# Later stores, later gate evictions and other queue places in the attention stage of a gated encoder block

## The chip, the cores and the metric

The kernel runs on one core of a Trainium2 chip. The metric is the device time of one execution in microseconds (us). The engines that matter are TensorE (PE: matmuls and transposes), its weight load (PEld), VectorE (DVE), ScalarE (ACT), GpSimd (POOL) and SyncE (SP, which only issues DMAs). Each works through its own instructions in the order in which they were written; an instruction waits on semaphores of other engines and of DMAs. DMAs are issued by SP and by ACT.

## The reference

One layer of an encoder block over 1024 positions of width 1024, in float32:

```
h = rmsnorm(x, g_mix) * (1 + scale1) + shift1          # shift, scale, gate from silu(c) @ w_ada + b_ada
proj = h @ w_in                                        # q, k, v of branches A and B, gates gA, gB
oa = mixture_of_dilations(qa, ka, va, rel_bias)        # A: 8 heads, three dilated windows each
ob = neighbourhood_attention_2d(qb, kb, vb, na_rpb)    # B: 8 heads, 8 x 16 window on a 16 x 64 grid
merged = sigmoid(ga) * (oa @ w_branch_dil) + sigmoid(gb) * (ob @ w_branch_na)
x = x + gate1 * (merged @ w_out)
h2 = rmsnorm(x, g_ffn) * (1 + scale2) + shift2
u = depthwise_conv(h2 @ w_up);  x = x + gate2 * ((gelu(u_gate) * u_val) @ w_down)
return rmsnorm(x, g_final)

# mixture_of_dilations: for each window, softmax attention with a bias, and its log-denominator;
w = softmax(stack(lses));  out = einsum(w, stack(outs))   # the windows' outputs are weighed and added
```

## The kernel before

Every float32 product is made of three matmuls on high and low parts, so an operand is split by a copy on ACT (the high part) and a subtraction on DVE or POOL (the low part). The changed part is the attention stage. It is written as 102 slots, a table from slot number and phase to jobs. In each slot the kernel first runs `settle` (ACT and DVE work that follows the previous slot's transposes and scores), then the phases "first" (loads and POOL work), "O" (probabilities times values), "T" (transposes of the probabilities), "S" (scores) and "last". PE, ACT, DVE, SP and POOL all take the order in which this is written.

Between the phases, `fill(n)` puts in n steps of the gate projection: three matmuls of 128x512 (L84 to L86) for one of 8 blocks of the contraction. Eight steps make a 128x512 tile `pj` in one of two PSUM banks; there are 32 such tiles, 256 steps. Twenty-one steps are left after the last slot; among them the next stage's operands are prepared (`o_split`, `first_split`): this is the seam. A tile's bank is free when ACT has copied it to `gs` (L1309); ACT then issues the store (L1310).

ACT and DVE work that needs no exact place stands in a list, `aside`. `catch_up` takes from it after each step, and `ensure(mark)` empties it up to a mark.

Branch A runs in slots 0 to 63 (`DilHead`, 8 slots a head, `DilPair` for two heads). Scores get a bias tile that POOL first adds `lnm` to (L853, L990). When a pair is done, its softmax statistics are turned, stored and read back in another layout (L1121 to L1129), factors are computed on DVE, stored (L1150, L1155), read back spread over positions (`fb`, L1162), the sums `u` are multiplied by them (`weigh`, L1167) and added (`merge`, L1176), and the result `oa` is stored (L1177). This runs beside later heads, for the last pair beside branch B.

Branch B (`NaHead`, 4 slots a head from slot 64) loads q and k (L401), values (L773) and a bias for each of three column blocks (L1218, `na_bias`). DVE adds it to the scores (L1240), ACT takes the exponential (L1242), DVE and POOL normalise halves (L1247, L1250), PE transposes (L1259) and multiplies (L1272), ACT and DVE add halves to `u` (L1281, L1285), and after two heads SP stores `ob` (L1287).

Each DMA is given one of eight semaphores in turn, in the program's order over both issuing engines, so an issue also waits for the DMA eight places before it.

Of the kernel before, what the change touches and what calls it, by code (L numbers as in the profile page):

```python
# [29 lines left out]
def hybrid_encoder(tc, xT, c, w_ada, small, w_in, p1_bias, p23_bias, na_bias, ln2_mult, ident, w_br, w_out,  # L30
# [61 lines left out]
    ps_g = tc.alloc_tile_pool(name="psg", bufs=2, space=PSUM)  # L92
    qkpool = tc.alloc_tile_pool(name="qk", bufs=4)

# [859 lines left out]
    slots = collections.defaultdict(lambda: {"first": [], "O": [], "T": [], "late O": [], "S": [], "last": [], "W": []})  # L954

    def at(slot, phase, job, *args):
        slots[slot][phase].append((job, args))

    class DilHead:
# [133 lines left out]
    class DilPair:  # L1093
        def __init__(self, pr):
            self.pr, s0 = pr, 16 * pr
            at(s0, "first", self.begin) if pr else self.begin()
            for i in range(2):
                DilHead(self, pr, i, s0 + 8 * i, lambda: self.u, lambda: self.st)
            at(s0 + 17, "T", self.turn)
            at(s0 + 20, "first", self.spread)  # L1100
            at(s0 + 22, "last", self.factors)
            at(s0 + 23, "last", self.shares)
            for z in range(2):
                at(s0 + 25 + z, "first", self.load, 1, z)
            for n, g, z in ((28, 1, 0), (29, 1, 1), (31, 0, 0), (32, 0, 1)):
                at(s0 + n, "last", self.weigh, g, z)
            at(s0 + 33, "first", self.merge)

# [31 lines left out]
        def shares(self):  # L1140
# [5 lines left out]
            for g in range(2):  # L1146
                dve.tensor_tensor(fa[:, g], fa[:, g], fl, OP.mult)
            to = f_scr[self.pr]
            for i in range(2):
# [14 lines left out]
        def weigh(self, g, z):  # L1164
            ensure(self.done)
            dst = self.u[g][:, 512 * z:512 * z + 512]
            dve.tensor_tensor(dst, dst, self.fb.pop((g, z)), OP.mult)  # L1167
            if g:
                self.load(0, z)

        def merge(self):
            u = self.u
            for z in range(2):
                dst = u[1].rearrange("p (r b j) -> p b r j", r=4, b=8)[:, 4 * z:4 * z + 4]
                src = u[0][:, 512 * z:512 * z + 512].rearrange("p (b r j) -> p b r j", b=4, r=4)
                pool.tensor_tensor(dst, dst, src, OP.add)  # L1176
            sp.dma_start(o_scr[0][self.pr], u[1])  # L1177

    na_col = [0, 576, 576, 1344]

    class NaHead:
        def __init__(self, head, s0):
# [7 lines left out]
            for n, cb in enumerate((0, 3, 1, 2)):  # L1190
                at(s0 + n - 1, "first", self.bias, cb)
                at(s0 + n, "S", self.scores, cb)
# [69 lines left out]
        def out(self, pair):  # L1262
# [20 lines left out]
            def two():  # L1283
                for dst, pv in parts:
                    dve.tensor_tensor(dst, pv[0:64], dst, OP.add)  # L1285
                if self.i and pair == (1, 2):
                    sp.dma_start(o_scr[1][self.head // 2], oT)  # L1287
            o_marks.append(aside(800, one, two))

    def fill_steps():  # L1290
        w, raw = first_w, {1: ahead.pop(25)}
        w_mark = 0
        marks = [0, 0]
        for n in range(16):
# [6 lines left out]
            for hf in range(2):  # L1301
                ensure(marks[-2])
                p = ps_g.tile([128, 512], FT, name="pj")
                for k in range(KT):
                    product(p, w, lambda k: h[hf, k], ks=[k])
                    if k == KT - 1:
                        def out(p=p, n=n, hf=hf):
                            g = gspool.tile([128, 512], FT, name="gs")
                            act.activation(g, p, AF.Copy)  # L1309
                            act.dma_start(g_scr[n][:, halves[hf]], g)  # L1310
                        aside(600, out)
                        marks.append(count[0])
                    yield
# [24 lines left out]
    att_sp.enter_context(tc.manual_schedule(engines={sp.engine}))  # L1338
    fill(5)
    for s in range(102):  # L1340
        n = 2 + (s % 4 == 3) if s < 64 else 2 + s % 2 if s < 96 else 1
        settle()
# [5 lines left out]
        run(slots[s]["last"])  # L1348
        fill(n - (n > 1))
    ensure(count[0])  # L1350
    sm_pool.release()
# [724 lines left out]
```

## Time and profile before

| | us |
|---|---|
| median of 3 runs (lowest to highest) | 1515.66 (1515.45 to 1517.59) |
| the profiled execution, its own time | 1514.76 |
| its span, first to last instruction | 1513.0 |
| PE busy | 1456.3 (96%) |
| DVE, ACT, POOL busy | 965.3, 792.8, 841.3 |
| mean granted clock of PE | 0.987 |
| attention stage, about | 277 to 677 |

How to read it: times are us from the span's start. In a table of windows each engine's busy time in a stretch stands with its count of instructions; the granted clock is PE's, and the DMA share is the packets' time over 16 DMA engines. In a list of waits a row names who waited, for whom, the total, how often, and the longest. In a timeline the brackets give the idle time of the engine just before an instruction and what ended it.

### The profile page before, as it was taken

What the parts mean: (1) busy time and instruction counts of PE and PEld (TensorE: products, weight loads), DVE (VectorE), ACT (ScalarE), POOL (GpSimd) and SP (SyncE); (2) the same over time, 40 slices, a digit from 0 to 9 for tenths busy, and PEclk for the clock granted to TensorE, in tenths of its full rate; (3) what the DMA queues carried; (4) which work ended last, traced back from release to release, by engine and by line L of the source; (5) the groups of instructions that cost most, each with busy time, mean ns of one, the idle gap of its engine ahead of it and who ended that gap; (6) DMA issues with size and microseconds to landing.
All of it is one profiled execution on the core that took longest, in us unless ns stands there. A gap on an engine that the chain in (4) does not pass through costs nothing.

```text
span 1513.0 us, 21241 instructions
## 1 busy us (share of the span) xinstructions
PE 1456.3 (96%) x7308; PEld 1230.2 (81%) x7308; DVE 965.3 (64%) x1809; ACT 792.8 (52%) x1479; POOL 841.3 (56%) x690
## 2 busy tenths in 40 slices
PE   9999999899999789999999999999999999999998
PEld 8877888788888678878888878888888888877888
DVE  7696543256655566656634898666666667787865
ACT  6635543377776456654335455444444447574542
POOL 4165675343342345522258858766666676988712
PEclk9999999999999889999999999999999999999999
DMA  9595355855687979558734412222222234532213
GB/s 369 200 349 200 108 188 204 213 144 148 150 220 210 232 189 265 167 192 274 248 134 153 140 55 98 84 84 85 84 84 84 84 127 142 202 124 80 101 48 112
DMA packets 130515, 241.13 MB, mean 159 GB/s; under 512 B 47812, under 2 KB 60740, under 8 KB 130372
## 3 DMA queue, kind: packets, MB, share of 16 engines
q1 hardware_dynamic: 117144, 211.65, 45.3%
q10 hardware_dynamic: 13264, 28.12, 5.0%
q8 instruction: 58, 0.95, 0.3%
q14 instruction: 49, 0.40, 0.1%
HBM read 185.60 MB, written 59.90 MB: 162 GB/s over the span
## 4 chain that ended last, share of the span: by engine, by line
PE 46%; DVE 3%; DMA 2%; POOL 2%; ACT 1%; issue 1%; SPq 0%; DVEq 0%; POOLq 0%; ACTq 0%
PE pj L495 10%; PE pj L496 10%; PE pj L497 10%; PE pj L86 5%; PE pj L84 5%; PE pj L85 5%; DMA wraw<-w_down 1%; DVE big L460 1%; POOL wsl L61 0%; DVE big L1705 0%; DMA oraw<-ob 0%; ACT wsh L57 0%; DVE op L1606 0%; POOL big L441 0%; ACT whi L57 0%
## 5 line engine op out<-in xcount | busy, mean ns | idle before, releaser
L61 POOL TENSOR_TENSOR wlo<-wraw,whi 128x512 fp32r<-128x512 f32 (+1 forms) x90 | 114.6, 1294 | 133.9 <-ACT whi L57 132.1
L495 PE MATMUL pj<-op,wsh 128*128 128x512 f32 x408 | 158.7, 390 | 2.8 <-ACT wsh L57 2.8
L496 PE MATMUL pj<-op,wsh 128*128 128x512 f32 x408 | 158.7, 389 | 0.5 <-DVE op L1495 0.5
L497 PE MATMUL pj<-op,wsl 128*128 128x512 f32 x408 | 157.4, 389 | 0.0
L61 POOL TENSOR_TENSOR wsl<-big,wsh 128x512 fp32r<-128x512 f32 (+1 forms) x86 | 111.7, 1320 | 44.4 <-ACT wsh L57 39.3
L84 PE MATMUL pj<-h,whi 128*128 128x512 f32 x272 | 118.7, 436 | 2.5 <-ACT gs L1309 2.5
L85 PE MATMUL pj<-h,whi 128*128 128x512 f32 x272 | 109.5, 403 | 0.0
L86 PE MATMUL pj<-h,wlo 128*128 128x512 f32 x272 | 109.4, 402 | 0.0
L1705 DVE SCALAR_TENSOR_TENSOR big<-pj,sm,big 128x512 f32<-128x512 f32 (+2 forms) x183 | 94.9, 563 | 16.5 <-ACT big L1699 15.6
L889 DVE TENSOR_TENSOR tl<-T,th 128x512 fp32r<-128x512 f32 (+3 forms) x120 | 76.3, 650 | 36.5 <-ACT th L885 36.2
L495 PEld LDWEIGHTS pj<-op,wsh 128*128 128x128 f32 x408 | 76.7, 188 | 19.6 <-ACT wsh L57 3.6
L495 PE MATMUL pj<-op,whi 128*128 128x512 f32 x232 | 90.6, 390 | 0.0
L496 PEld LDWEIGHTS pj<-op,wsh 128*128 128x128 f32 x408 | 76.7, 188 | 16.8 <-DVE op L1495 0.9
L497 PE MATMUL pj<-op,wlo 128*128 128x512 f32 x232 | 90.3, 389 | 0.0
L496 PE MATMUL pj<-op,whi 128*128 128x512 f32 x232 | 90.3, 389 | 0.0
L497 PEld LDWEIGHTS pj<-op,wsl 128*128 128x128 f32 x408 | 76.6, 188 | 16.1 <-POOL wsl L61 0.2
L61 POOL TENSOR_TENSOR wsl<-wraw,wsh 128x384 fp32r<-128x384 f32 (+1 forms) x46 | 56.6, 1251 | 57.6 <-ACT wsh L57 50.0
L1250 POOL TENSOR_SCALAR P<-P,stb 128x288 f32<-128x288 f32 (+1 forms) x32 | 41.5, 1297 | 67.8 <-DVE stb L1247 33.4
L875 DVE CUSTOM_DVE_ANT_0 P<-S,bias 128x256 f32<-128x256 f32 x128 | 48.9, 419 | 46.5 <-PE S L1006 33.7
L57 ACT ACTIVATE whi<-wraw 128x1024 fp32r<-128x1024 f32 (+2 forms) x48 | 47.4, 992 | 58.6 <-PE pj L85 33.5
L876 ACT ACTIVATE P<-P,st 128x256 f32<-128x256 f32 x128 | 63.9, 501 | 23.4 <-DVE st L875 22.9
L885 ACT ACTIVATE th<-T 128x512 fp32r<-128x512 f32 (+3 forms) x120 | 65.2, 561 | 20.4 <-ACT gs L1309 5.7
(476 smaller groups left out, 4536.1 us busy)
## 6 DMA issues: line engine op xcount, KB each, us to landing
wada<-w_ada SPq DMA_DIRECT2D x31, 512.0 KB
qks<-qs ACTq DMA_DIRECT2D x28, 512.0 KB
wraw<-w_in SPq DMA_DIRECT2D x24, 512.0 KB
big<-w_up SPq DMA_DIRECT2D x22, 512.0 KB
wraw<-w_up SPq DMA_DIRECT2D x22, 512.0 KB
big<-as SPq DMA_DIRECT2D x22, 512.0 KB
as<-big SPq DMA_DIRECT2D x21, 512.0 KB
qs<-qks SPq DMA_DIRECT2D x32, 256.0 KB
```

What stands on the lines that cost most here:

```text
L61: lo_eng.tensor_tensor(lo[:, i:i + step], raw[:, i:i + step], f(hi)[:, i:i + step], OP.subtract)
L84: pe.matmul(psum, whi[:, k0 + k], mhi, start=k == 0, stop=False)
L85: pe.matmul(psum, whi[:, k0 + k], mlo, start=False, stop=False)
L86: pe.matmul(psum, wlo[:, k0 + k], mhi, start=False, stop=k == n - 1)
L495: pe.matmul(psum, whi[:, k], bhi, start=j < 4 and k == 0, stop=False, skip_group_check=True)
L496: pe.matmul(psum, whi[:, k], blo, start=False, stop=False, skip_group_check=True)
L497: pe.matmul(psum, wlo[:, k], bhi, start=False, stop=k == n - 1, skip_group_check=True)
L875: dve.tensor_tensor_reduce(pp, d, bias, -1.0, BIG, OP.add, OP.min, mi)
L876: act.activation(pp, pp, AF.Exp, bias=mi, scale=-1.0, accum_out=li)
L885: act.activation(tt[0][:m, :n], pt[:m, :n], AF.Copy)
L889: dve.tensor_tensor(tt[1][:m, :n], pt[:m, :n], f(tt[0])[:m, :n], OP.subtract)
L1705: dve.scalar_tensor_tensor(y[:, dst], src, wt, y[:, dst], OP.mult, OP.add)
```

## The change

Seven edits, all in the attention stage.

- `fill(5)` before slot 0 becomes `fill(11)`. In slots 64 to 95 three steps instead of two are given in every third slot, where it was every second. The sum up to the seam stays at 235.
- A finished gate tile is held, and its copy is put on the list after the second step of the next tile (for the last tile at once). Its store goes from ACT to SP, one slot later.
- The stores of `ob` and `oa` are issued one slot after the additions that they store.
- The stores of the factors become a job of their own (`send`), at the start of the next slot.
- Both `fb` loads of a pair's first half come together in slot 26 of the pair (they were in 25 and 26); weighing moves from DVE to POOL, and each weighing and the merge come one slot earlier. The second half's loads come a slot after the weighing that frees the buffer.
- Branch B's bias loads come one slot earlier.
- The pool `qk`, whose space the first head's tiles take over, is given reuse by tile.

```diff
-    qkpool = tc.alloc_tile_pool(name="qk", bufs=4)
+    qkpool = tc.alloc_tile_pool(name="qk", bufs=4, reuse_waits="tile")
...
+    LAST = 101
+    now = [0]
+    def later(n, job):
+        if now[0] + n > LAST:
+            job()
+        else:
+            at(now[0] + n, "first", job)
...
             at(s0 + 23, "last", self.shares)
+            at(s0 + 24, "first", self.send)
             for z in range(2):
-                at(s0 + 25 + z, "first", self.load, 1, z)
-            for n, g, z in ((28, 1, 0), (29, 1, 1), (31, 0, 0), (32, 0, 1)):
+                at(s0 + 26, "first", self.load, 1, z)
+            for n, g, z in ((27, 1, 0), (28, 1, 1), (30, 0, 0), (31, 0, 1)):
                 at(s0 + n, "last", self.weigh, g, z)
-            at(s0 + 33, "first", self.merge)
+            at(s0 + 32, "first", self.merge)
...
-            to = f_scr[self.pr]
+
+        def send(self):
+            to, fa = f_scr[self.pr], self.fa
...
-            dve.tensor_tensor(dst, dst, self.fb.pop((g, z)), OP.mult)
+            pool.tensor_tensor(dst, dst, self.fb.pop((g, z)), OP.mult)
             if g:
-                self.load(0, z)
+                later(1, lambda: self.load(0, z))
...
-            sp.dma_start(o_scr[0][self.pr], u[1])
+            later(1, lambda: sp.dma_start(o_scr[0][self.pr], u[1]))
...
-                at(s0 + n - 1, "first", self.bias, cb)
+                at(s0 + n - 2, "first", self.bias, cb)
...
-                    sp.dma_start(o_scr[1][self.head // 2], oT)
+                    later(1, lambda: sp.dma_start(o_scr[1][self.head // 2], oT))
...
-        marks = [0, 0]
+        marks, held = [0, 0], []
+        def out(p, n, hf):
+            g = gspool.tile([128, 512], FT, name="gs")
+            act.activation(g, p, AF.Copy)
+            later(1, lambda: sp.dma_start(g_scr[n][:, halves[hf]], g))
+        def release():
+            while held:
+                args = held.pop()
+                marks.append(aside(600, lambda: out(*args)))
...
-                ensure(marks[-2])
+                ensure(marks[2 * n + hf])
...
+                    if k == 1:
+                        release()
                     if k == KT - 1:
-                        def out(p=p, n=n, hf=hf):
-                            g = gspool.tile([128, 512], FT, name="gs")
-                            act.activation(g, p, AF.Copy)
-                            act.dma_start(g_scr[n][:, halves[hf]], g)
-                        aside(600, out)
-                        marks.append(count[0])
+                        held.append((p, n, hf))
+                        if n == 15 and hf:
+                            release()
...
-    fill(5)
-    for s in range(102):
-        n = 2 + (s % 4 == 3) if s < 64 else 2 + s % 2 if s < 96 else 1
+    fill(11)
+    for s in range(LAST + 1):
+        now[0] = s
+        n = 2 + (s % 4 == 3) if s < 64 else 2 + (s % 3 == 0) if s < 96 else 1
...
+    now[0] = LAST + 1
     ensure(count[0])
```

How the instructions move is shown at two places. The first is SP's queue around the bias loads of the first branch B head. Before (a row is line, operation, destination and source, shape, and a count of equal rows):

```order
L1162 DMA fb<-fcs 64x1x512 x2
L65 DMA wraw<-w_in 128x1024
L1218 DMA bias<-na_bias 128x576 x2
L401 DMA qs<-qks 64x1024 x2
L401 DMA ks<-qks 64x1024 x2
L401 DMA kl<-qks 64x1024 x2
L1177 DMA oa<-u_3791 128x1024
L1218 DMA bias<-na_bias 128x768
L1121 DMA sts<-fr 64x128
```

Now:

```order
L1310 DMA gs<-gs 128x512
L1174 DMA fb<-fcs 64x1x512 x2
L1230 DMA bias<-na_bias 128x576 x2
L1230 DMA bias<-na_bias 128x768
L401 DMA qs<-qks 64x1024 x2
L401 DMA ks<-qks 64x1024 x2
L401 DMA kl<-qks 64x1024 x2
L1310 DMA gs<-gs 128x512
L1189 DMA oa<-u_3821 128x1024
L1131 DMA sts<-fr 64x128
```

The head's third bias stands ahead of the next head's q and k and of the store of `oa`, where it stood behind them; the gate stores (`gs`) are now among SP's issues.

The second place is ACT at the seam, where `o0hi` and `o1hi` are the high parts of the attention outputs and `whi` those of the first branch weights. Before:

```order
L1281 ACTIVATE u_6561<-O 64x16x4x4 x4
L1372 ACTIVATE o0hi<-oraw 128x512 x4
L57 ACTIVATE whi<-wraw 128x1024
L1309 ACTIVATE gs<-pj 128x512
L1310 DMA gs<-gs 128x512
L1372 ACTIVATE o1hi<-oraw 128x512 x3
L1378 ACT_TABLE_LOAD
```

Now:

```order
L1293 ACTIVATE u_6562<-O 64x16x4x4 x2
L1395 ACTIVATE o0hi<-oraw 128x512 x4
L57 ACTIVATE whi<-wraw 128x1024
L1395 ACTIVATE o1hi<-oraw 128x512 x2
L1309 ACTIVATE gs<-pj 128x512
L1395 ACTIVATE o1hi<-oraw 128x512
L1401 ACT_TABLE_LOAD
```

The copy of the gate tile stands behind two of the `o1hi` splits, where it stood ahead of all three, and its store is no longer on ACT.

## The prediction

> **What bounds the kernel now.** I read the busy table first: TensorE (PE) is busy for 96% of the span, so time can come only from PE's idle time and from stretches where its clock is cut. Three stretches hold the attention stage (columns: span; busy PE, PE weight load, DVE, ACT, POOL; granted clock; DMA share; GB/s):
> ```profile
> 277.00:490.00 213.00, 199.15 (x1240) 174.99 (x1239) 118.19 (x390) 145.62 (x401) 80.95 (x77) 0.99 0.69 182
> 490.00:630.00 140.00, 117.98 (x690) 103.94 (x689) 84.83 (x250) 82.19 (x221) 66.87 (x58) 0.91 0.86 224
> 630.00:677.00 47.00, 43.48 (x252) 37.58 (x250) 25.86 (x60) 29.08 (x65) 18.16 (x16) 0.96 0.46 160
> ```
> PE idles 13.9, 22.0 and 3.5 us there. The list of waits says for whom:
> ```profile
> PE T L1259 <- DVE tl L889: 11.7, 6, 4.7
> PE T L1115 <- DVE tl L889: 8.0, 3, 6.2
> PE T L1021 <- ACT P L876: 5.5, 1, 5.5
> PE pj L84 <- ACT gs L1309: 2.5, 1, 2.5
> ```
> Few waits, long ones. Windows laid around the longest show what follows each:
> ```profile
> 283.00:295.00 12.00, 6.52 (x32) 5.16 (x31) 2.85 (x13) 5.87 (x17) 9.50 (x11) 0.86 0.98 242
> 496.00:510.00 14.00, 7.84 (x33) 6.57 (x32) 5.18 (x16) 4.24 (x12) 2.36 (x2) 0.76 0.95 247
> 526.00:537.00 11.00, 5.99 (x25) 4.96 (x23) 5.69 (x20) 3.56 (x10) 2.18 (x2) 0.69 0.51 102
> 550.00:561.00 11.00, 6.96 (x30) 6.03 (x30) 6.22 (x18) 7.13 (x19) 4.96 (x4) 0.69 0.86 240
> 610.00:620.00 10.00, 8.11 (x46) 7.36 (x45) 4.36 (x14) 7.36 (x20) 7.92 (x7) 0.83 0.81 220
> 668.00:678.00 10.00, 7.54 (x27) 6.02 (x27) 5.84 (x9) 8.66 (x13) 2.51 (x2) 0.83 1.04 392
> ```
> Length times (1 - clock) is what the cut clock costs: 1.7, 3.4, 3.4, 3.4, 1.7 and 1.7 us, 15.3 in all. With 39.4 us of idle time, about 55 us of the 400 could be had. Nothing outside the stage is edited.
>
> Next, what each wait hangs on. The three in the neighbourhood heads (timeline: start, duration, engine, [idle before <- releaser]):
> ```profile
> 491.17 0.83 SPq L1218 DMA_DIRECT2D bias<-na_bias  x2
> 500.88 0.46 DVE L1240 CUSTOM_DVE_ANT_0 P<-S,bias 128x288 f32<-128x288 f32 x1 [4.11 <-DMA bias<-na_bias]
> 502.47 0.39 PE L1115 MATMUL T<-idt,st 128*64 128x128 f32 x1 [6.16 <-DVE tl L889]
> 529.23 0.56 DVE L1240 CUSTOM_DVE_ANT_0 P<-S,bias 128x384 f32<-128x384 f32 x1 [4.41 <-DMA bias<-na_bias]
> 531.02 1.09 PE L1259 MATMUL T<-idt,P 128*128 128x128 f32 x4 [4.68 <-DVE tl L889]
> 543.99 0.46 SPq L1218 DMA_DIRECT2D bias<-na_bias  x1
> 552.42 0.56 DVE L1240 CUSTOM_DVE_ANT_0 P<-S,bias 128x384 f32<-128x384 f32 x1 [6.61 <-DMA bias<-na_bias]
> 554.22 1.08 PE L1259 MATMUL T<-idt,P 128*128 128x128 f32 x4 [4.04 <-DVE tl L889]
> ```
> All three are one thing. The bias lands 9.7 us (491.17 to 500.88) or 8.4 us (543.99 to 552.42) after its issue; DVE stands on it with the low halves (tl) of the next transposes queued behind; PE waits for those.
>
> **The change part by part.** *Start.* Six product steps move ahead of slot 0. PE's first step and the next start here, and its last matmul before the stall is followed by the wait for the first head's bias:
> ```profile
> 276.70 0.39 PE L84 MATMUL pj<-h,whi 128*128 128x512 f32 x1
> 277.38 0.39 PE L84 MATMUL pj<-h,whi 128*128 128x512 f32 x1
> 283.59 0.39 PE L86 MATMUL pj<-h,wlo 128*128 128x512 f32 x1
> 285.50 0.99 POOL L853 TENSOR_TENSOR bias<-bias,lnm 128x384 f32<-128x384 f32 x1 [10.30 <-DMA bias<-p_bias]
> 289.44 1.39 PE L1021 MATMUL T<-idt,P 128*128 128x128 f32 x4 [5.46 <-ACT P L876]
> ```
> A step is 0.68 us (276.70 to 277.38), six are 4.1. PE's work ahead of the stall ends 4.1 us later, at about 288 instead of 284, while the bias (285.50, then DVE and ACT) still sets 289.44. The stall shrinks to 1.4 us and its clock loss of 1.7 goes too: gain 5.8. Bounds: 4.1 if the clock still falls, 7.2 if nothing of the stall is left. The pool's reuse by tile adds nothing to this: with it and without it, all five engines have the same instructions with the same waits, so those loads start no earlier.
>
> *Gate stores off ACT, copies two steps later.* Twice ACT, with its copy done, stands at the store it has to issue:
> ```profile
> 380.66 0.33 ACTq L1310 DMA_DIRECT2D gs<-gs  x1
> 381.03 0.60 ACT L885 ACTIVATE th<-T 128x512 fp32r<-128x512 f32 x1 [2.39 <-DMA fb<-fcs]
> 381.68 0.38 PE L1033 MATMUL O<-th,vv 128*128 128x256 f32 x1 [1.00 <-ACT th L885]
> 485.83 0.33 ACTq L1310 DMA_DIRECT2D gs<-gs  x1
> 485.85 0.69 DVE L1167 TENSOR_TENSOR u<-u,fb 128x512 f32<-128x512 f32 x1 [4.33 <-DMA fb<-fcs]
> 486.20 0.60 ACT L885 ACTIVATE th<-T 128x512 fp32r<-128x512 f32 x1 [2.86 <-DMA fb<-fcs]
> 486.85 0.38 PE L1033 MATMUL O<-th,vv 128*128 128x256 f32 x1 [1.48 <-ACT th L885]
> 488.72 0.39 PE L1033 MATMUL O<-tl,vv 128*128 128x256 f32 x1 [1.49 <-DVE tl L889]
> ```
> ACT was held 2.39 and 2.86 us by an fb load that has no part in the copy. With the store on SP, and the weighing (which held DVE 4.33 us at the same place) on POOL, these 1.0, 1.48 and 1.49 us go: gain 4.0. The first stretch's other idle time is 13.9 - 5.5 - 4.0 = 4.4 us; some is ACT waiting for a product's last matmul before its copy, which two more steps cover. I take half, 2.2 (bounds 0 and 4.4).
>
> The Trainium skill, DMA: Bandwidth & Descriptors, section "Issuing engines are not separate DMA queues", says that DMAs of several engines run on the same 16 DMA engines, and that issuing from several saves only issue time. By that rule the move buys no transfer speed and puts 32 issues of 0.33 us, 10.6 us, on the queue that also issues the bias; were all of that on the path, an estimate from that page's rule is 1499 us. The rows above show ACT paying for being held and not for issuing, so the sum goes without it.
>
> *Weighing and merge.* Sixteen multiplies leave DVE for POOL:
> ```profile
> L1167 DVE TENSOR_TENSOR u<-u,fb 128x512 f32<-128x512 f32 x16 | 12.2, 760 | 9.3 <-DMA fb<-fcs 9.3
> L1176 POOL TENSOR_TENSOR u<-u,u 128x512 f32<-128x512 f32 x8 | 10.3, 1282 | 11.1 <-DVE u L1167 11.1
> ```
> At the merge's 1.28 us each they take 20.5 us of POOL, which is busy 66.9 of 140 us in the fullest stretch: hidden. If that cover is gone, behind a late fb stand POOL's half of the normalising and weight splits; DVE's wait of 4.33 plus 1.28, at the two near-path weighings of the last pair, would cost up to 11.
>
> *Neighbourhood heads.* Their bias loads go one slot earlier; stores of u and the factors leave SP a slot later. 102 slots between 277 and the seam (about 660) are 3.7 us each, so the first two waits for the bias (4.11, 4.41) nearly vanish and the third leaves 2.9. What limits the heads then is read from the steady part:
> ```profile
> 560.00:600.00 40.00, 38.99 (x252) 34.65 (x251) 27.88 (x82) 27.56 (x74) 25.83 (x22) 1.00 1.01 252
> ```
> Here the DMA engines are full and PE just keeps up, with 2.5% idle. All of 490 to 630 holds 0.86 x 140 = 120 us of DMA work, which the change moves hardly at all: at most 20 us to gain. PE's own floor is lower: 118.0 busy less 12.6 for the clock (0.09 x 140), less the 4.1 us of steps moved ahead, 101 us: 39 to gain. The lower end is no gain. I take 17: the DMA floor plus 2.5% of 120, since the row with full DMA engines is the nearest to what comes.
>
> *Seam.* After the last slot, ACT's copy that frees PE's bank now comes behind two more splits (order rows above):
> ```profile
> 668.79 1.04 ACT L57 ACTIVATE whi<-wraw 128x1024 fp32r<-128x1024 f32 x1
> 670.93 1.67 ACT L1372 ACTIVATE o1hi<-oraw 128x512 fp32r<-128x512 f32 x3 [0.48 <-DMA wraw<-w_br]
> 670.50 0.50 PE L84 MATMUL pj<-h,whi 128*128 128x512 f32 x1 [2.46 <-ACT gs L1309]
> ```
> Two splits at 1.67 / 3 are 1.1 us, with some of the 0.48 about 1.3: a loss. SP's store of that copy stands ahead of the next w_br load and later oraw loads; if those come late too, I allow a second wait of the present 2.46: a loss of about 4. No gain is in it, since nothing on ACT's way to the copy is taken away. The TensorE: Matmul & The Clock Gate page of the Trainium skill ("What's actually happening") puts the half clock behind an idle window of about 3.4 us; this seam already loses its clock after 2.46 us, so the trace differs. By the page the loss would grow by another 1.7 us and the estimate be 1490; by the row it is paid already.
>
> *Sum.* 5.8 + 4.0 + 2.2 + 17 - 1.3 = 27.7. The profiled execution took 1514.76 us (span 1513.0 and 1.8 around it), 0.9 under the median of the runs, 1515.66. So 1515.7 - 27.7 = **1488 us**.
>
> **The rivals.** *PE's floor* (0.15): the DMA share counts the packets' own time, which lengthens when transfers crowd, so full need not mean at the limit; against it, 1.01 beside PE at 97%. Gain 39 in place of 17: 1466.
>
> *Bias as late as before* (0.12): DMA latency grows by what the slot gives. For it: 9.7 us of latency in full stretches. Against it: 526 to 537 has a DMA share of 0.51 while a stall lasts, so the queue, not the engines, was late. Then the heads gain nothing and lose the cover of the moved steps: 5.8 + 4.0 + 2.2 - 1.3 - 4.1 = 6.6, 1509.
>
> *A gate store at the head of SP's queue* (0.09, slower): it waits there for ACT's copy, and behind it wait a head's bias and q/k loads. Each such delay of over a slot brings back DVE's 4.4 us and 3.4 of clock, 7.8 us; in all eight heads 62, where 25.1 (14.9 idle, 10.2 clock) stand now: 37 worse, less the 10.7 gained elsewhere, 1542. It decides from five heads on ((25.1 + 10.7) / 7.8 = 4.6). Against it: the store is put a slot after its copy.
>
> **How the numbers follow.** My forecast has 0.60, the rivals 0.15, 0.12 and 0.09, and 0.04 is for no change at all. The forecast's own range is 1478 (all of the small waits, 25 in the heads) to 1502 (8 in the heads, the lower bounds elsewhere, seam 2.6). With the rivals, 1469 to 1509 leaves out about 2 in 10. About 0.2%, 3 us, can be told from no change. Faster: 0.60 + 0.15 + nearly all of 0.12, 0.86; same 0.05; slower 0.09.
>
> **What would show it.** Right: no DVE wait for na_bias over 2 us, the stall before the first transposes under 2 us with full clock, no ACT wait on fb, 490 to 630 shorter by 14 to 20 us with the DMA share near 1, the seam's wait at 3 to 4 us. Wrong: half-clock stretches still in the heads, SP idle on a gate copy with bias loads behind it, POOL waiting on fb with PE behind its P, or a DMA share well under 1 with PE at 100% (then PE's floor).

## The result and the profile after

The changed kernel takes 1506.81 us (median of nine runs, 1499.74 to 1511.88) beside 1515.65 for the kernel before (nine runs, 1511.87 to 1518.27): a ratio of 0.9935, 95% interval 0.9914 to 0.9957. It is 8.8 us faster, where 28 were forecast. The profiled execution of the changed kernel took 1502.23 us, span 1500.1, so it is one of its faster ones, 4.6 under the median; numbers from its trace are made against that time, 12.5 under the 1514.76 of the profiled execution before. Of all executions in this document one, of c3_vb_early, was in a slow state (2053.53 us); it is left out of every number.

The three stretches of the attention stage in the changed kernel (columns as before: span; busy PE, PE weight load, DVE, ACT, POOL; granted clock; DMA share; GB/s):
```profile
277.00:490.00 213.00, 205.33 (x1291) 181.46 (x1289) 114.16 (x391) 150.94 (x413) 99.26 (x92) 1.00 0.74 193
490.00:630.00 140.00, 125.58 (x768) 111.25 (x769) 89.06 (x275) 92.43 (x248) 81.57 (x73) 0.94 0.82 215
630.00:677.00 47.00, 37.91 (x170) 29.43 (x171) 19.34 (x29) 20.60 (x34) 5.87 (x5) 0.96 0.61 206
```
PE idles 7.7, 14.4 and 9.1 us (before 13.9, 22.0 and 3.5). The windows are the same, but work has moved through them: what was at 670 is now at 651. The third row is where something was given back. PE's timeline of the changed kernel names the waits (start, duration, instruction, and in brackets the idle time before it and what ended it):
```profile
288.08 0.33 PE L1030 MATMUL T<-idt,P 128*128 128x128 f32 x1 [1.43 <-ACT P L876]
...
490.76 0.39 PE L1125 MATMUL T<-idt,st 128*64 128x128 f32 x1 [5.38 <-DVE tl L889]
...
539.29 1.09 PE L1271 MATMUL T<-idt,P 128*96 128x128 f32 x4 [5.96 <-POOL P L1262]
...
650.83 0.50 PE L84 MATMUL pj<-h,whi 128*128 128x512 f32 x1 [3.53 <-ACT gs L1309]
...
669.56 0.75 PE L84 MATMUL pj<-o1hi,whi 128*128 128x512 f32 x1 [2.20 <-ACT o1hi L1395]
```
The start's wait of 5.46 is 1.43, the two waits of the first stretch on ACT and DVE (1.48, 1.49) are gone, and so is the wait of 4.68 at 531. The first head's wait (6.16) stands at 5.38. New are two waits on POOL's half of the normalising, 5.96 and, at 559.86, 3.03, and the waits behind the seam, 1.10 at 662.45 and 2.20.

Two landmarks tell how the 12.5 us came about. At the copy that frees PE's bank at the seam the changed kernel is 19.7 us ahead (650.83 against 670.50). A group of eight small matmuls stands behind the seam in all three kernels below; first the kernel before, then the changed one, then the changed kernel with the seam's stores on ACT (an experiment below):
```profile
721.33 0.26 PE L197 MATMUL pbc<-oraw 128*32 128x12 f32 x8
```
```profile
708.75 0.26 PE L197 MATMUL pbc<-oraw 128*32 128x12 f32 x8 [0.51 <-DVE oraw L185]
```
```profile
702.59 0.25 PE L197 MATMUL pbc<-oraw 128*32 128x12 f32 x8
651.77 0.50 PE L84 MATMUL pj<-h,whi 128*128 128x512 f32 x1 [3.52 <-ACT gs L1309]
```
From the one landmark to the other it is 50.83 us before, 57.92 in the changed kernel and 50.82 in the experiment. The changed kernel loses 7.1 us there. The further runs below bear this out: with the seam's stores on SP the stretch takes 59.2 (e1) and 58.9 (e4), and 49.4 to 52.6 in every kernel with these stores on ACT but one (b1, 55.7).

### The profile page after: what moved, and what is told of

The parts are those of the page before. It is cut to its first block, busy times and chain, and to the rows that moved or that the text cites. A ratio compares the mean times of both kernels' runs of the same rounds, so it can differ in the third digit from the quotient of the medians.

```text
span 1500.1 us, 21296 instructions
## 1 busy us (share of the span) xinstructions
PE 1451.6 (97%) x7308; PEld 1223.7 (82%) x7308; DVE 950.5 (63%) x1793; ACT 793.9 (53%) x1479; POOL 859.2 (57%) x706
## 4 chain that ended last, share of the span: by engine, by line
PE 41%; DVE 7%; DMA 4%; ACT 2%; issue 1%; POOL 1%; SPq 1%; DVEq 0%; ACTq 0%; POOLq 0%
PE pj L495 10%; PE pj L496 10%; PE pj L497 10%; PE pj L86 3%; PE pj L84 3%; PE pj L85 3%; DMA wraw<-w_down 1%; DVE op L1629 1%; DMA oraw<-w_ada 1%; DMA oraw<-oa 1%; DVE op L1548 1%; DMA big<-as 1%; DVE big L460 1%; ACT op L1547 1%; DVE x L1598 1%
## 5 line engine op out<-in xcount | busy, mean ns | idle before, releaser
L1722 ACT ACTIVATE big<-pj,sm 128x512 f32<-128x512 f32 x61 | 47.0, 773 | 54.6 <-DVE pj L516 32.2
L516 DVE TENSOR_TENSOR pj<-pj,wc 128x512 f32<-128x512 f32 x40 | 27.8, 696 | 73.3 <-PE pj L497 73.3
```

## The experiments

Each difference is that of two medians, of 4 to 12 runs of the edited kernel and 9 to 23 of the kernel before beside it on the same chip; the ratio and its 95% interval come from the same runs. "Gates on ACT at the seam" (e2_seam_act) became the base of the later ones.

| label | edit | ratio (interval) | us |
|---|---|---|---|
| (the change) | | 0.9935 (0.9914 to 0.9957) | -8.8 |
| e2_seam_act | change, seam's stores on ACT | 0.9870 (0.9851 to 0.9889) | -20.6 |
| e1_weigh_dve | change, weighing on DVE | 0.9943 (0.9925 to 0.9962) | -9.0 |
| e3_both | e1 and e2 | 0.9890 (0.9871 to 0.9908) | -18.8 |
| e4_bias_early | change, first head's bias two slots earlier | 0.9920 (0.9904 to 0.9936) | -12.8 |
| c2_weigh_late | e2, weighing later on POOL | 0.9861 (0.9835 to 0.9887) | -20.4 |
| c3_vb_early | e2, layout of values ten slots earlier | 0.9850 (0.9823 to 0.9877) | -23.3 |
| c4_late_early | c2 and c3 | 0.9855 (0.9829 to 0.9881) | -20.3 |
| d1_dve_late | e3, weighing two and three slots later | 0.9846 (0.9823 to 0.9869) | -24.6 |
| f5_values | d1, head's values one slot earlier | 0.9866 (0.9839 to 0.9893) | -19.7 |
| d2_send_act | e2, factors stored from ACT | 1.0032 (1.0018 to 1.0047) | +4.8 |
| d3_late_send | d1 and d2 | 1.0015 (1.0001 to 1.0029) | +2.0 |
| d4_no_start | e2, the six moved steps put back | 0.9865 (0.9841 to 0.9888) | -21.3 |
| b1_start | before, with the six moved steps alone | 1.0046 (1.0028 to 1.0063) | +8.2 |
| f1_gates | before, with later copies and SP's stores alone | 0.9935 (0.9915 to 0.9956) | -10.1 |
| b2_bias | before, with the earlier bias loads alone | 0.9942 (0.9921 to 0.9963) | -8.3 |

### The seam's stores

```diff
-            later(1, lambda: sp.dma_start(g_scr[n][:, halves[hf]], g))
+            if now[0] + 1 > LAST:
+                act.dma_start(g_scr[n][:, halves[hf]], g)
+            else:
+                later(1, lambda: sp.dma_start(g_scr[n][:, halves[hf]], g))
```


> The changed kernel with one part undone at the seam alone: the gate copies made after the last slot are stored from ACT's queue again, all earlier ones from SP's; the copies stay two steps late. Theory A: behind the seam SP stands on a store whose copy is not made, with the w_br load and the loads of oraw and gates behind it; those loads come up to 10 us late, and this makes the waits at 662 to 677 (1.10, 0.23, 2.20, 0.68 and 0.62 us, 4.8 in all) and a half clock of 1.7. With the stores on ACT these go: 5 to 7 us faster than the changed kernel, the loads issued before the copy ends, the wait of 3.53 for ACT's copy itself unchanged. Theory B: the loads are late because the merge and the last stores before them land late: then SP still idles, ACT's splits wait as now, and the time is within 2 us.

Measured: 1492.82 beside 1513.43, 20.6 us under before. SP's queue at the seam, in the changed kernel:
```profile
642.37 0.91 SPq L1394 DMA_DIRECT2D oraw<-ob  x2
650.80 0.32 SPq L1310 DMA_DIRECT2D gs<-gs  x1
651.22 0.38 SPq L65 DMA_DIRECT2D wraw<-w_br  x1
...
664.91 0.32 SPq L1310 DMA_DIRECT2D gs<-gs  x1
665.33 1.98 SPq L1394 DMA_DIRECT2D oraw<-ob  x3
```
and with those stores on ACT:
```profile
644.29 0.51 SPq L65 DMA_DIRECT2D wraw<-w_br  x1
...
654.28 4.51 SPq L1397 DMA_DIRECT2D oraw<-ob  x4
```
SP issues nothing from 643.3 to 650.80: at the head of its queue is the store of a copy that ACT makes only at the end of its splits. The weight load goes out 6.9 us later, the seven `oraw` loads behind it 2 to 5, and the last three, behind the second store, about nine. What then waits is ACT, for `oraw`, and PE behind ACT. In ACT's timeline of the changed kernel:
```profile
656.74 0.63 ACT L1395 ACTIVATE o1hi<-oraw 128x512 fp32r<-128x512 f32 x1 [5.96 <-DMA oraw<-ob]
...
668.88 1.29 ACT L1395 ACTIVATE o1hi<-oraw 128x512 fp32r<-128x512 f32 x2 [4.00 <-DMA oraw<-ob]
```
With the stores on ACT, PE waits for none of this; the wait for the copy itself stays (3.52). Theory A holds, though it gave 5 to 7 us. The traces explain 7.1 of the 11.8 us by which the differences to before differ (9.8 between e1 and e3 below). The rest is not shown to be the seam's: from the eight matmuls to the end, which no edit touches, the traces differ by up to 4 us (787.6 to 791.7), and e1's, with the stores on SP, is as short there as e2's.

### Who weighs

```diff
-            pool.tensor_tensor(dst, dst, self.fb.pop((g, z)), OP.mult)
+            dve.tensor_tensor(dst, dst, self.fb.pop((g, z)), OP.mult)
```


> The changed kernel with one part undone: the sixteen weighings are on DVE again; their slots, the merge and all else stay. Theory A: the two new stalls of the neighbourhood heads (PE waits 5.96 and 3.03 us for POOL's P L1262, with half clock behind both, 3.4 and 1.7 us: 14.1 in all) come from POOL's weighing, which waits for fb with POOL's half of the normalising queued behind. With the weighing on DVE those two waits go; DVE may stand on fb for 2 to 3 us in their place. 6 to 12 us faster than the changed kernel, no PE wait for POOL P over 2 us. Theory B: late transfers in full DMA engines set the pace of the heads, whichever engine stands on them: the stalls come back as PE waits for DVE tl, and the time is within 3 us of the changed kernel's 1506.8.

> The weighing back on DVE and the seam's stores back on ACT, both in the changed kernel. If theory A holds for both and they do not touch each other (they lie 90 us apart), the gains add: 11 to 19 us faster than the changed kernel, 1488 to 1496, which is where the prediction stood. If late transfers set the pace, it is the better of the two alone.

Measured: 9.0 us under before for e1, where the change is 8.8 under; 18.8 for both edits, where the seam's alone gives 20.6. Theory A falls. In the changed kernel POOL stood on fb, with PE's `P` behind it (POOL's timeline):
```profile
536.99 1.26 POOL L1179 TENSOR_TENSOR u<-u,fb 128x512 f32<-128x512 f32 x1 [8.19 <-DMA fb<-fcs]
```
In e1_weigh_dve DVE stands on the same transfer, with the reciprocals behind it (DVE's and PE's timeline):
```profile
544.05 0.69 DVE L1179 TENSOR_TENSOR u<-u,fb 128x512 f32<-128x512 f32 x1 [7.04 <-DMA fb<-fcs]
```
```profile
547.35 1.06 PE L1271 MATMUL T<-idt,P 128*96 128x128 f32 x4 [6.66 <-DVE stb L1259]
```
PE waits 6.66 where it waited 5.96. What is late is fb, not the engine that uses it.

### The wait that stays: order in the heads

Six runs move something that is late in the heads out of the way.

```diff
e4  -                at(s0 + n - 2, "first", self.bias, cb)
e4  +                at(s0 + n - (2 if head else 4), "first", self.bias, cb)
c2  -            for n, g, z in ((27, 1, 0), (28, 1, 1), (30, 0, 0), (31, 0, 1)):
c2  +            for n, g, z in ((28, 1, 0), (29, 1, 1), (32, 0, 0), (33, 0, 1)):
c3  -    for n, cb in zip((54, 56, 59, 61), (0, 3, 1, 2)):
c3  +    for n, cb in zip((44, 46, 48, 50), (0, 3, 1, 2)):
d1  +            for n, g, z in ((29, 1, 0), (30, 1, 1), (33, 0, 0), (34, 0, 1)):
f5  -            at(s0 + 2, "first", self.load)
f5  +            at(s0 + 1, "first", self.load)
```


> The changed kernel with the first neighbourhood head's bias loads two more slots earlier, ahead of eight transfers of branch values and two pairs of fb loads; all other heads as they are. Theory A: the first head's stall (PE 5.38 us on DVE tl, half clock 3.4, behind DVE's 7.50 us wait for the bias) is a matter of order in SP's queue: the wait falls to under 2 us and 4 to 9 us are gained. Theory B: between 470 and 500 the DMA engines are 98% busy, so what is moved ahead only makes the next load late (fb or the values): another wait of 4 to 8 us stands within 15 us behind it, and the time is within 3 us of the changed kernel.

> The changed kernel with the seam's stores on ACT (e2_seam_act) and the four weighings of a pair one, one, two and two slots later (28, 29, 32, 33 in place of 27, 28, 30, 31; merge at 34 in place of 32), on POOL as in the change. Putting the weighing on DVE moved the stall from POOL to DVE and left the time, so the engine is not the cause. Theory A: the cause is the slots: the change loads fb one slot later and weighs one slot earlier, which leaves about one slot (3.7 us) for loads that take up to 10 us (issued at 526.8, landed at 537.0). With the slots given back, PE's waits of 6.3 and 3.2 us for POOL's P and the half clock behind them (6.8 and 3.4 us at half speed, 5.1 lost) go: 8 to 14 us faster than e2_seam_act, 1479 to 1485. Theory B: the DMA engines' volume sets the pace of the heads: the wait comes back on a bias or a q/k load, and the time is within 3 us of e2_seam_act's 1492.8.

> e2_seam_act with the sixteen transfers that lay out the branch values for the neighbourhood heads (v<-vbc, 256 KB each) about ten slots earlier (44, 46, 48, 50 in place of 54, 56, 59, 61); nothing else. Theory A: the first head's bias is late because those transfers crowd the DMA engines and SP's queue just ahead of it (share 0.91 to 1.04 from 470 to 500, against 0.48 from 440 to 450); earlier they lie beside a half idle DMA, DVE's wait of about 8 us for the first bias falls under 2, PE's stall of 6.5 us and its half clock of 6.8 us go: 6 to 10 us faster than e2_seam_act, 1483 to 1487. Theory B: the first bias is late for its own place in the order (behind fb loads that wait for POOL): the stall stays, and the time is within 3 us of 1492.8, or worse if the early transfers now delay a dilated head's loads.

> Both edits, c2_weigh_late and c3_vb_early, together. If both of their theories A hold, the gains add: 1466 to 1478, with PE's idle time between the first and the last head under 8 us. If the DMA volume sets the pace, no better than the better one of the two alone.

> e3_both (weighing on DVE, seam's stores on ACT) with the weighings of a pair two and three slots later (29, 30, 33, 34 in place of 27, 28, 30, 31; merge at 35). POOL's order is not set by the slots (the scheduler left its first weighing of the last pair ahead of the same P in c2_weigh_late), DVE's is; so this is the first run in which the weighing itself moves. Theory A, too few slots between the fb load and its use: DVE's wait of 7.0 us for fb lies two slots (7.4 us) later and is covered; PE's wait of 7.0 us on DVE stb goes, with its half clock of 6.8 us: 7 to 11 us faster than e3_both's 1494.7, 1484 to 1488. Theory B, every transfer of that stretch lands late (values 6 us and a bias 3 us late beside fb): PE still waits 3 us or more near 540, now behind ACT's copy of the values or DVE's wait for a bias, and the gain is under 4 us.

> d1_dve_late with each neighbourhood head's values loaded one slot earlier, ahead of the weight and fb loads. In d1_dve_late the weighing no longer stands in the way near 549, and PE's wait of 7.4 us there now ends with the head's values (ACT waits 5.7 us for vv, POOL and DVE behind it). If order in the queue is what counts, that wait falls under 3 us and 4 to 8 us are gained on d1_dve_late's 1490.8 (1483 to 1487). If the stretch's transfers are simply more than it has time for, the next one in line (fb or a bias) is late by the same amount, and the time is within 3 us.

In c3_vb_early and c4_late_early the early layout of branch B's values overwrites rows that the last dilated heads have yet to load, so part of the output is not the reference's; the instructions and transfers are the same ones.

*The first head.* With its bias two slots earlier (e4) PE's single wait of 5.38 becomes two:
```profile
496.36 0.69 PE L1242 MATMUL S<-ks,qs 128*128 128x384 f32 x1 [3.96 <-DVE stb L1252]
507.42 0.61 PE L1271 MATMUL T<-idt,P 128*96 128x128 f32 x4 [3.75 <-DVE tl L889]
```
That is theory B in the trace. The medians (12.8 under before, the change 8.8) have overlapping intervals, so a gain of some us is neither shown nor excluded. With the sixteen layout transfers out of the stretch (c3) the first head's wait does go (the largest near it is 1.26, at 500.75), and c3's trace is 5 us shorter than e2's; but the times lie 23.3 and 20.6 us under before with overlapping intervals, so here too a gain of some us is neither shown nor excluded. Theory A's 6 to 10 is not borne out: c4, which lacks that wait as well, is no faster than c2 (20.3 and 20.4 under before).

*The wait near 540.* It stands under every edit of this group, but what ends it changes. Three kernels, each with PE's row and what the engine ahead of it waited for (from the list of waits between 520 and 548, or 560): with the weighing later on POOL (c2):
```profile
544.07 1.09 PE L1271 MATMUL T<-idt,P 128*96 128x128 f32 x4 [6.53 <-POOL P L1262]
POOL u L1179 <- DMA fb<-fcs: 8.7, 1, 8.7
```
with the weighing on DVE and really later (d1):
```profile
549.39 0.85 PE L1271 MATMUL T<-idt,P 128*96 128x128 f32 x3 [7.37 <-DVE tl L889]
ACT vv L779 <- DMA vv<-v: 8.2, 3, 5.7
```
and with the values ahead of that (f5):
```profile
548.27 1.06 PE L1271 MATMUL T<-idt,P 128*96 128x128 f32 x4 [7.84 <-DVE tl L889]
DVE P L1252 <- DMA bias<-na_bias: 13.4, 2, 10.2
```
First fb, then the values, then a bias; PE waits 6.5, 7.4 and 7.8 us. c2 moved nothing there: POOL's instructions at this place kept their order, since only PE, ACT, DVE and SP take theirs from the table of slots. (What stands ahead of the prediction on POOL's order is wrong in this.) d1, where the weighing did move, is the fastest of all against before (24.6), 5.8 more than e3, and its interval just misses e3's: by the times the later slots gain something, between the 7 to 11 of theory A and the under 4 of theory B. Where, its trace does not show: it is that of its slowest execution (1496.14, as f5's 1499.41 is), has the wait undiminished, and is 2.5 us longer than e3's. f5, which differs from d1 by one slot of the values, is 19.7 under before. In these three traces the order of the transfers only passes the wait on.

### SP's issuing

Three rows of what SP issues ahead of that wait in the changed kernel:
```profile
517.16 0.97 SPq L1162 DMA_DIRECT2D fcs<-fa  x2
518.18 3.82 SPq L1167 DMA_DIRECT2D fcs<-fa  x8
...
530.63 5.61 SPq L773 DMA_DIRECT2D vv<-v  x4
```
Added up from 497 to 545, such rows take 43.6 of the 48 us, and 28.8 in the kernel before. But a row joins like issues from the start of the first to the end of the last, with what lies between: the four loads of the values last 0.33 to 0.38 us each, 1.4 of the 5.61. One by one, the issues last 33.5 us, and 25.9 before; for the rest of its rows SP stands between two issues, each of which also waits for the DMA eight places before. So the 43.6 that the next expectation takes for issuing is too much. The ten small stores of the factors are spread over 4.9 us, and the DMA share, 1.00 from 517 to 520, falls while the last of them go out (window of the changed kernel; the last two numbers are share and GB/s):
```profile
520.00:523.00 3.00, 3.00 (x25) 2.86 (x24) 2.59 (x9) 2.44 (x8) 2.17 (x3) 1.00 0.25 32
```
So the stores were given to ACT:
```diff
-                sp.dma_start(to[1, i].rearrange("c (x j) -> x c j", j=32),
+                act.dma_start(to[1, i].rearrange("c (x j) -> x c j", j=32),
...
-                    sp.dma_start(near[i, r], fa[32 * i + 8 * r:32 * i + 8 * r + 8, 0:1].to_broadcast([8, 8, 32]))
+                    act.dma_start(near[i, r], fa[32 * i + 8 * r:32 * i + 8 * r + 8, 0:1].to_broadcast([8, 8, 32]))
```


> e2_seam_act with the ten small stores of a pair's factors (fcs<-fa, 8 to 32 KB each) issued by ACT in place of SP; weighing on POOL and its slots as in the change. In the changed kernel SP issues for 43.6 of the 48 us from 497 to 545 (28.8 before), and while it issues those ten stores the DMA engines fall to a tenth of their rate. Theory C, SP's issuing time is the limit there: fb is issued 4 to 5 us earlier, POOL's wait of 8 us for it and PE's of 6.3 us shrink by 4 to 5, half of the half clock goes: 5 to 8 us faster than e2_seam_act's 1492.8, 1485 to 1488. Theory B, the bytes are the limit: fb lands as late as now, within 3 us. ACT pays 10 issues of 0.33 us each per pair; if ACT is held at them by a late factor or transfer, PE waits for th instead and it is slower by up to 4.

> d1_dve_late and d2_send_act together. If the slots and SP's issuing each carry a part, it is the fastest of all, 1478 to 1485; if both only move the same wait, it is as the better one of the two.

Measured: 4.8 and 2.0 us slower than before, 25 and 27 slower than their bases e2 and d1. In d2_send_act PE waits once for each pair (4.80 and 5.73 for the first two; the third and fourth are shown), and ACT's timeline, the stores' own line (shortest, median and longest issue in ns) and ACT's list of waits say why:
```profile
487.50 0.48 PE L1095 MATMUL O<-th,vv 128*128 128x128 f32 x1 [6.22 <-ACT th L885]
...
555.24 1.06 PE L1271 MATMUL T<-idt,P 128*96 128x128 f32 x4 [11.60 <-DVE tl L889]
```
```profile
359.58 5.79 ACTq L1167 DMA_DIRECT2D fcs<-fa  x7
...
L1167 ACTq DMA_DIRECT2D fcs<-fa x32: 270/274/1100, 357.8 to 552.3; - x32
...
ACT vv L779 <- DMA fcs<-fa: 32.4, 3, 13.9
```
A store takes ACT 0.27 us to issue, but the seven are spread over 5.79 us: between two of them ACT stands for the DMA eight places before, one of its own or of SP's, and its next instructions wait up to 13.9 us behind such stores. The wait of 6.26 near 540 in e2 is 11.60 here. The expectation priced a held ACT at up to 4 us; it costs 25, and it hides whatever SP gained. So the run does not tell theory C from theory B: whether bytes, SP's issuing or the waits between its issues make the heads' transfers late stays open. It does show in the large what the prediction read from the gate stores of the kernel before, an ACT that stands at an issue for a DMA that has no part in it.

### The six steps ahead of the first slot

```diff
-    fill(5)
+    fill(11)
...
-        n = 2 + (s % 4 == 3) if s < 64 else 2 + s % 2 if s < 96 else 1
+        n = 2 + (s % 4 == 3) if s < 64 else 2 + (s % 3 == 0) if s < 96 else 1
```


> The kernel before with one part of the change alone: six product steps moved ahead of the first slot, six fewer in the heads. By the prediction the wait of 5.5 us before the first transposes shrinks to 1.4 and its half clock goes, 5.8 us faster. But the six steps (4.1 us) then lack in the heads, where they covered waits: by the change's trace only 1.2 to 1.7 us of it shows at 300 us, and the rest must show as fewer steps later. Theory A: it shows there in full: 4 to 6 us faster than before. Theory B: in the heads PE waits for transfers and not for itself, so the steps taken away there come back as longer waits: 1 to 2.5 us faster, with waits in the heads 3 to 4 us longer in sum.

> e2_seam_act with the six product steps that the change moves ahead of the first slot put back in the heads; all else as in e2_seam_act. In the kernel before, those steps alone made it 8 us slower, but there the scheduler also put a weight load ahead of the first head's q/k loads; here SP's order up to the first slot is unchanged, so this is the clean test. By the prediction the steps are worth 5.8 us: about 1498.6. If the heads are paced by transfers, PE's six steps there cost nothing (they cover waits) and only the start's stall counts: the start 1.7 us worse in its clock and 0 to 2 us gained or lost in the heads: 1492 to 1496.

Alone in the kernel before (b1) they make it 8.2 us slower. There, the scheduler also placed a second weight load ahead of the first head's q/k loads, and it stood at the head of SP's queue for most of 18 us (SP's and PE's timeline of b1_start):
```profile
256.99 18.42 SPq L65 DMA_DIRECT2D wraw<-w_in  x2
```
```profile
288.39 0.35 PE L1006 MATMUL S<-kl,qs 128*128 128x256 f32 x1 [2.91 <-DMA kl<-qks]
294.93 0.33 PE L1021 MATMUL T<-idt,P 128*128 128x128 f32 x1 [1.83 <-ACT P L876]
```
So the start's wait was not shortened but moved, and b1 is no clean price of the steps; neither theory named this. Its trace is 2.5 us late at the seam (672.99 against 670.50) and loses another 4.8 behind it, for a reason that stays open. Putting the steps back in e2_seam_act (d4) is one: the wait at the start is back, and PE's wait at the seam still ends about as early (650.83, in e2_seam_act 651.77):
```profile
287.91 1.39 PE L1030 MATMUL T<-idt,P 128*128 128x128 f32 x4 [5.29 <-ACT P L876]
```
The median is 21.3 us under before, with the steps moved 20.6: no difference. Six steps fewer in the heads leave longer waits there (the first head's 3.83 in d4 against 6.54 in e2, the one near 540 3.13 against 6.26).

### Two parts alone

f1_gates takes the gate part of the change into the kernel before, with the seam's stores on ACT; b2_bias takes this line alone:
```diff
-                at(s0 + n - 1, "first", self.bias, cb)
+                at(s0 + n - 2, "first", self.bias, cb)
```


> The kernel before with one part of the change alone: gate copies two steps later and their stores from SP one slot after the copy, but from ACT at the seam as in e2_seam_act. Bias, factors, weighing, merge and the steps ahead of the first slot stay as before. The prediction gave this part 4.0 us (ACT and DVE held by an fb load: 1.0, 1.48, 1.49 of PE's waits) and 2.2 for smaller waits: 1509 if that is all of it. By the runs so far the changed kernel without the seam's fault is 21 us under before, and neither the moved steps nor the engine of the weighing carry any of it; if the stores carry most of it (an ACT that stands at its stores also delays copies, splits and with them SP's loads), this part alone gives 10 to 16 us: 1499 to 1505. If SP is the limit in the heads, the stores that it now issues cost there: 1512 or more.

> The kernel before with one part of the change alone: each neighbourhood bias is loaded one slot earlier. The prediction gave the heads 17 us, nearly all from this edit. If that holds alone: 1498 or less, with DVE's waits for na_bias (4.1, 4.4 and 6.6 us) gone but for 2.9. If what is late is the stretch's transfers and not their place in the order, the wait passes to the q/k loads and values that now stand behind the biases: 1511 to 1516, no gain beyond 4 us.

Measured: 10.1 and 8.3 us. PE's waits in the heads and at the seam, with the one just ahead of the heads, first of f1, then of b2 (before: 1.48 and 1.49 ahead of the heads, then 6.16, 4.68, 4.04 and 2.46):
```profile
484.06 0.58 PE L1042 MATMUL O<-tl,vv 128*128 128x256 f32 x1 [4.04 <-DVE tl L889]
498.02 0.39 PE L1124 MATMUL T<-idt,st 128*64 128x128 f32 x1 [3.94 <-DVE tl L889]
525.67 1.09 PE L1268 MATMUL T<-idt,P 128*128 128x128 f32 x4 [4.62 <-DVE tl L889]
546.47 0.63 PE L1268 MATMUL T<-idt,P 128*128 128x128 f32 x4 [2.82 <-DVE tl L889]
659.44 0.50 PE L84 MATMUL pj<-h,whi 128*128 128x512 f32 x1 [3.65 <-ACT gs L1306]
```
```profile
488.64 0.38 PE L1033 MATMUL O<-th,vv 128*128 128x256 f32 x1 [2.89 <-ACT th L885]
505.90 0.30 PE L1069 MATMUL T<-idt,P 128*128 128x128 f32 x1 [1.91 <-DVE tl L889]
532.50 0.61 PE L1259 MATMUL T<-idt,P 128*96 128x128 f32 x4 [2.41 <-DVE stb L1247]
548.70 0.63 PE L1259 MATMUL T<-idt,P 128*128 128x128 f32 x4 [2.53 <-DVE tl L889]
663.12 0.70 PE L84 MATMUL pj<-h,whi 128*128 128x512 f32 x1 [2.42 <-ACT gs L1309]
```
They reach the seam 11.1 and 7.4 us ahead of before; added up 18.4, and the changed kernel, with both, is 19.7 ahead. (Of f1's and of the changed kernel's lead 1.2 us is there before the stage begins, at SP's first weight load of 256 to 257.) So the two parts would account for nearly all of the gain; no run has just these two, and the later factors and `fb` loads were not run alone. Each expectation lies beside its result: f1 is at the low end of its 10 to 16, half of the gain and not most; b2 lies between its two theories, more than 4 and half of 17. In b2, ACT is still held ahead of the heads (2.89), and all three waits of the heads are shorter. In f1, DVE still waits for biases in the heads (3.96, 3.52, 5.38; before 4.11, 4.41, 6.61), and two of the three waits are shorter; ahead of the heads ACT is no longer held, but DVE stands on `fb` for 5.24, and PE's wait there is longer than before.

## Why the prediction was wrong

The direction was right and 1506.81 lies in the range; the size was not. By its own terms:

| term | predicted | measured, and by what |
|---|---|---|
| start | 5.8 | -0.6 (e2 against d4), not told from nothing |
| stores off ACT, small waits | 4.0 + 2.2 | 10.1 (f1) |
| weighing on POOL | 0, up to 11 lost | -0.2 (the change against e1), not told from nothing |
| neighbourhood heads | 17 | 8.3 (b2) |
| seam | -1.3, at worst -4 | -11.8 (the change against e2), 7.1 of it traced |
| sum | 27.7 | 5.8; the change itself 8.8 |

**The seam is the step that failed by most.** The prediction named the mechanism, SP's store "ahead of the next w_br load and later oraw loads", but left it out of the sum and priced it, at worst, with the wait that stood there before, 2.46, as though it could come only once. The price could have been read from the queues of the kernel before (SP's and ACT's timeline):
```profile
664.13 0.52 SPq L65 DMA_DIRECT2D wraw<-w_br  x1
669.85 0.60 ACT L1309 ACTIVATE gs<-pj 128x512 f32<-128x512 f32 x1
```
The weight load goes out at 664.13, and the copy that the store must wait for ends at 670.45, 6.3 us later; ten of the sixteen `oraw` loads stand behind it. The rival "a gate store at the head of SP's queue" was this mechanism at another place: it looked for it in the heads and set against it that the store is put a slot after its copy, but behind the last slot `later` puts it at once. The rest was right: the copy's own wait went from 2.46 to 3.53, 1.1 for the two splits, as worked out.

**The start was counted twice.** The wait shrank to 1.43, as forecast (1.4). But 4.1 of the 5.8 were steps that PE does earlier, which come back only as fewer steps in the heads, and the 17 for the heads was already a stretch paced by transfers in which PE's own work does not count. By the prediction's own view of the heads, the start is worth its clock, 1.7, and the sum 23.6. Even that did not show at the seam: the changed kernel has full clock from 283 to 295 and d4 has 0.72, and d4's longer start is made good by shorter waits in the heads.

**The heads' 17 is the term that was mis-sized.** It took all three waits for one thing, a bias a slot too late, and let the DMA floor stand as the next limit. The heads did not come to that floor: from 490 to 630 the changed kernel has a DMA share of 0.82 (0.86 before) with PE idle for 14.4 us. The earlier bias removes some of the waits (8.3), but what is late is a whole train of transfers. When the bias is early, fb is late; when fb has time, the values are late; when those are early, a bias is. The rival "bias as late as before" was right for the first head alone, 7.50 us of DVE's wait in the changed kernel; it gave 1509, and came out nearest for other reasons. Against it the prediction held that "the queue, not the engines, was late"; the runs do not decide between the two, but either way a place one slot earlier passes part of the lateness on.

**The gate part was undersized, and gained mostly elsewhere than where it was priced.** It was priced by the two rows where ACT is seen to be held by an fb load. No row of f1 or of the changed kernel has that any more, but in f1 the waits of 1.48 and 1.49 became one of 4.04, behind a DVE that stands on an `fb` load. f1 is 4.5 us ahead of before at the first head's wait (498.02 against 502.47) and 11.1 at the seam: more than half of its gain is made in the heads and behind them, where waits of 6.16 and 4.04 became 3.94 and 2.82. Whether the later copies or an ACT free of stores does it is not shown.

**The weighing** did what the bound said, POOL waiting for fb with PE behind `P`, and the prediction listed that among the signs of being wrong. But e1 shows that the move to POOL is not the cause, so the 9 us seen there (5.96 and 3.03) would be a wrong price for it. Of the signs of being right, the start's (1.43, full clock), ACT's on fb and the seam's (3.53) came true; the one that the heads hang on, no DVE wait for a bias over 2 us, did not (7.50 and 2.42).

On the rule that DMAs of several engines share the same 16 DMA engines (the Trainium skill, DMA: Bandwidth & Descriptors, "Issuing engines are not separate DMA queues"): no run here tests it, since in the one that moved ten issues of a pair from SP to ACT the 25 us lost hide what the transfers did. The page also calls the time of issuing usually small beside the transfer; here an issue of a store of 8 KB took ACT 0.27 us, and what counted was not that but ACT's standing between the issues.

## What to carry to other kernels

A store in an in-order queue costs what stands behind it, so price a moved store by the loads behind it and by how late its data is, above all where a loop ends and a delay of "one slot later" has no slot left; keep the old queue there. A row of a timeline that joins several issues holds the waits between them; read the single issue before taking the row for time of issuing. Where several transfers in a stretch are late together, removing the one that is waited for shows the next, so a wait that one of them ends is no measure of what its edit will give; run that edit alone. Work moved from a stretch that waits into one that is full of waits elsewhere is no gain until the second stretch has been shown to be bound by that work.

## What was not expected of the hardware

A wait of 3.53 us at the seam of the changed kernel cost no clock, and one of 3.52 at the same place with the stores on ACT did (windows of the two, granted clock before the last two numbers):
```profile
648.00:657.00 9.00, 6.17 (x27) 5.11 (x28) 3.88 (x4) 3.01 (x6) 2.97 (x2) 1.00 0.51 161
```
```profile
648.00:657.00 9.00, 5.48 (x18) 4.15 (x17) 6.54 (x8) 7.88 (x11) 2.96 (x2) 0.81 1.04 395
```
0.19 x 9 is 1.7 us. Before, a wait of 2.46 there cost the same. The changed kernel lost as much (0.14 x 12) further on, where its longest wait is the 2.20:
```profile
664.00:676.00 12.00, 8.50 (x27) 5.58 (x26) 5.78 (x9) 5.15 (x8) 1.62 (x2) 0.86 0.73 234
```
So the length of a wait alone does not tell whether the clock falls.
